# Weight pieces split three ahead from two raw buffers, and gate products turned through four PSUM banks

## The chip, the core and the metric

The kernel runs on one core of a Trainium2 chip. The metric is device time in microseconds (us) from launch to end. The engines are TensorE (PE, its weight loads PEld), VectorE (DVE), ScalarE (ACT), GpSimd (POOL) and SyncE (SP, which here only issues DMAs). Lines such as L1178 are lines of the kernel before.

## What is computed

The reference is one layer of a decoder block for 256 tokens and 2048 channels, in float32. After a projection by `w_in` come retention and dilated attention, merged by gates and `w_out`; then cross attention on 256 memory tokens; then an expert layer in which each token picks, for each of 8 heads, 16 of 16384 experts by product keys:

```python
def expert_block(args):
    x_, i_, g_ = args
    u = u_tab[i_]
    a = jax.nn.gelu(jnp.einsum('td,tkd->tk', x_, u), approximate=False)
    return jnp.einsum('tk,tkd->td', a * g_, v_tab[i_])
```

`u_tab` and `v_tab` have 16384 rows of 2048 channels. The result is normalized once more.

## The kernel before, in words

**The stream.** All weights come as a stream of 464 pieces of 128 x 4 x 512 float32 (1 MiB). Pieces 0 to 207 belong to the projections and the memory layer, 208 to 335 to the table u, 336 to 463 to the table v: the kernel does not gather the experts of 192 of its tokens, but multiplies all 16384 rows of u by the tokens (`u_chunk`, L904), takes the Gelu, multiplies by a dense matrix G of gates, and multiplies by all rows of v (`v_group`, L989). The other 64 tokens are done by gathering rows (`lanes`, L811): per row of 128 lanes an indirect DMA on POOL (L835) and one DVE instruction (L843 for u, L861 for v), three fetches ahead.

**How a piece is fed.** Float32 products are made from two float32r parts. A piece lands in one of `RAW_BUFS` = 3 buffers `raw`, by a DMA that SP issues (`load_to`, L1162). ACT casts it to `hi` (L1177), DVE subtracts `lo` = raw - hi (L1178). These two have three buffers each, as the pool `stream` has. Three matmuls per block (`mm3`, L210 to L212) use `hi`, `lo` and the split activations; where the 64 tokens are left out, two of them make the second half (L916, L917, L1026, L1027). A piece of the first kind has 24 matmuls, one of u or v 20. `ahead(n)` (L1170) splits up to piece n + 2 before piece n's matmuls are written, and behind each split of a piece i stands the load of piece i + 3.

**The order of the work** is the order in which this Python code issues it: every engine and every DMA queue runs its instructions in that order. Side work consists of generators. `tick()` (L126) lets each of them go on by credits; from the routing on it is called twice per piece, after the second block of matmuls and after the piece, so a tick is half a piece.

**Gate products.** `weigh` (L929) is such a generator. Its items are, for each of 32 chunks of 512 experts, one of kind "a" (128 tokens) and for every second chunk one of kind "b" (64 tokens, two chunks side by side). Per item it loads a block of G and a block of activations `act` on SP's queue (L939 to L944, five items ahead), multiplies them on DVE (L969, two steps ahead), transposes four blocks on TensorE into one PSUM bank (L974), casts the bank on ACT (L977, L981), and a step later subtracts on DVE (`low`, L950, L955), which empties the bank. The bank comes from the tag `tp`, which has two. The tag `sm` has two more, which other parts use earlier (attention, scores, the matrix G). The result is one buffer of the pool `units`, which has `N_UNITS` = 30 buffers of 4 KB for nearly everything. `v_group` waits until the results of its chunk are there. Results for the table v may run eight chunks ahead of it, and so they are made in bursts, from the last quarter of one group of v pieces into the next group.

**The start** (L1183 to L1203) loads and splits the first `RAW_BUFS` pieces by quarters (`quarters`, L1159), with the split of x's quarter i beside piece i, and x's last quarter after them.

Of the kernel before, what the change touches and what calls it, by code (L numbers as in the profile page):

```python
# [10 lines left out]
F32R = mybir.dt.float32r  # L11
# [9 lines left out]
KQ = 4  # L21
# [8 lines left out]
N_EXP = N_KEYS * N_KEYS  # L30
N_CH = N_EXP // 512
V_GROUPS = (4, 8, 8, 8, 4)
RAW_BUFS = 3
SPLIT_AHEAD = 2
N_UNITS = 30
LANES = slice(64, 128)
LOW = slice(0, 64)
TICK = 4.0
LOADS = 5
# [36 lines left out]
def block_kernel(ctx, tc, a, out):  # L76
    nc = tc.nc
    ctx.enter_context(tc.manual_schedule())
    cp = ctx.enter_context(tc.tile_pool(name="consts", bufs=1))
    st = ctx.enter_context(tc.tile_pool(name="stream", bufs=3))  # L80
    up = ctx.enter_context(tc.tile_pool(name="units", bufs=N_UNITS))
    wp = ctx.enter_context(tc.tile_pool(name="work", bufs=4))
    sp = ctx.enter_context(tc.tile_pool(name="small", bufs=2))
# [3 lines left out]
    def unit(shape, dt=F32):  # L87
        return up.tile([128] + shape, dt, tag="unit", name="unit")
# [4 lines left out]
    def bank(tag, shape):  # L93
        return ps.tile([128] + shape, F32, tag=tag, name=tag, bufs=4 if tag == "acc" else 2)
# [77 lines left out]
    def split_sb(raw, gi, kq, ks=range(4), into=None):  # L172

        hi, lo = into or (unit([4, T], F32R), unit([4, T], F32R))
        for k in ks:
            g = gains[:, gi, 4 * kq + k:4 * kq + k + 1]
            nc.scalar.activation(hi[:, k], raw[:, k], AF.Copy, scale=g)
            nc.vector.scalar_tensor_tensor(lo[:, k], raw[:, k], g, hi[:, k], op0=OP.mult, op1=OP.subtract)
        return hi, lo
# [69 lines left out]
    x_T = [None] * KQ  # L249
    sm = {}  # L250

    def load_xT(kq):
        raw = unit([4, T])
        nc.sync.dma_start(raw, a["xT"][kq])
        return raw
# [376 lines left out]
    hf_T = [None] * 4  # L632
# [268 lines left out]
    v_at = [0]  # L901
# [27 lines left out]
    def weigh():  # L929

        while len(g_done) < 2:
            yield
        items = [(kind, c) for c in range(N_CH) for kind in ("a", "b")[:1 + c % 2]]
        w, turned = {}, {}

        def load(kind, c):
            t = unit([2, 512])
            if kind == "a":
                nc.sync.dma_start(t[:, 0], G_d[0][:, c * 512:c * 512 + 512])  # L939
                nc.sync.dma_start(t[:, 1], ga.pop(c))  # L940
            else:
                nc.sync.dma_start(t[LOW, 0], G_d[1][:, c * 512 - 512:c * 512])
                nc.sync.dma_start(t[LANES, 0], G_d[1][:, c * 512:c * 512 + 512])
                nc.sync.dma_start(t[:, 1], gb.pop(c // 2))  # L944
            w[kind, c] = t

        def low(kind, c):
            o, tp = turned.pop((kind, c))
            if kind == "a":
                nc.vector.tensor_sub(o[:, 1], tp, o[:, 0])  # L950
                A_T[c] = o
            else:
                both = tp.rearrange("p k (c t) -> p c k t", c=2)
                for j in range(2):
                    nc.vector.tensor_sub(o[:, j, :, 64:128], both[:, j], o[:, j, :, 0:64])  # L955
                B_T[c // 2] = o

        yield
        yield
        for i in range(LOADS):  # L960
            load(*items[i])
        for i in range(-3, len(items) + 1):
            if 0 <= i - 1:
                low(*items[i - 1])
            while i + LOADS < len(items) and 0 <= i and items[i][1] > v_at[0] + (1 if hf_T[0] is not None else 8):
                yield
            if 0 <= i + 2 < len(items):
                t = w[items[i + 2]]
                nc.vector.tensor_mul(t[:, 1], t[:, 1], t[:, 0])  # L969
            if 0 <= i < len(items):  # L970
                t = w.pop(items[i])
                tp = bank("tp", [4, 128])
                for k in range(4):
                    nc.tensor.transpose(tp[:, k], t[:, 1, k * 128:k * 128 + 128], ident)  # L974
                o = unit([2, 4, 128], F32R)
                if items[i][0] == "a":
                    nc.scalar.copy(o[:, 0], tp)  # L977
                else:
                    both = tp.rearrange("p k (c t) -> p c k t", c=2)
                    for j in range(2):  # L980
                        nc.scalar.copy(o[:, j, :, 0:64], both[:, j])  # L981
                turned[items[i]] = o, tp
            if LOADS <= i + LOADS < len(items):
                while items[i + LOADS][1] not in ga and items[i + LOADS][0] == "a" or items[i + LOADS][0] == "b" and items[i + LOADS][1] // 2 not in gb:
                    yield
                load(*items[i + LOADS])
            yield
# [134 lines left out]
    def route():  # L1122
# [5 lines left out]
        yield from gate_matrix()  # L1128
    call(lambda: add(route()))
    call(lambda: add(weigh(), 1))  # L1130
    call(lambda: add(lanes_in()))

# [22 lines left out]
    stream = [e for e in prog if e[0] is not None]  # L1155
# [3 lines left out]
    def quarters(i):  # L1159
        return [slice(k, k + 1) for k in range(KQ)] if i <= RAW_BUFS else [slice(0, KQ)]  # L1160

    def load_to(m):  # L1162
        while at["load"] < min(m, len(stream)):
            i = at["load"]
            raws[i] = st.tile([128, KQ, 512], F32, name="raw", bufs=RAW_BUFS)
            for ks in quarters(i):
                nc.sync.dma_start(raws[i][:, ks], stream[i][0][:, ks])
            at["load"] += 1

    def ahead(n):  # L1170
        while at["split"] < min(n + SPLIT_AHEAD + 1, len(stream)):
            i = at["split"]
            load_to(i + RAW_BUFS)
            raw = raws.pop(i)
            hi, lo = st.tile([128, KQ, 512], F32R, name="hi"), st.tile([128, KQ, 512], F32R, name="lo")
            for ks in quarters(i):
                nc.scalar.copy(hi[:, ks], raw[:, ks])  # L1177
                nc.vector.tensor_sub(lo[:, ks], raw[:, ks], hi[:, ks])  # L1178
            parts[i] = (hi, lo)
            at["split"] += 1  # L1180
            load_to(i + 1 + RAW_BUFS)

    raw_x = []  # L1183
    for i in range(RAW_BUFS):
        raw_x.append(load_xT(i))
        raws[i] = st.tile([128, KQ, 512], F32, name="raw", bufs=RAW_BUFS)
        for k in range(KQ):
            nc.sync.dma_start(raws[i][:, k], stream[i][0][:, k])
    at["load"] = RAW_BUFS
    raw_x.append(load_xT(3))  # L1190
    for i in range(RAW_BUFS):
        raw = raws.pop(i)
        hi, lo = st.tile([128, KQ, 512], F32R, name="hi"), st.tile([128, KQ, 512], F32R, name="lo")
# [6 lines left out]
        parts[i] = hi, lo  # L1200
        at["split"] = i + 1
        load_to(i + 1 + RAW_BUFS)
    x_T[3] = split_sb(raw_x[3], 0, 3)  # L1203
    n = 0
    for ap, fn in prog:
        if ap is None:
# [99 lines left out]
```

## Time and profile before

| | |
|---|---|
| median of three runs | 2597.49 us (2588.37 to 2598.75) |
| the profiled execution, its own time | 2592.94 us |
| its span, first to last instruction | 2591.0 us |
| mean granted TensorE clock | 0.990 of full speed |
| bytes moved by DMA | 700.50 MB, 270 GB/s over the span |
| SBUF of `raw`, `hi`, `lo` and `units`, per partition | 9 x 8 KB and 30 x 4 KB |

The profile is of one execution. An engine is busy while it runs an instruction; waiting and issuing DMAs are not counted. In a row of grouped instructions stand line, engine, operation, tile written <- tiles read, count, then busy us and mean ns of one, then the engine's idle time just before them and what ended it. A wait reads "engine, line <- what ended it: us in total, times, longest". A row of DMA issues gives count, size and the median us from issue to landing.

### The profile page before, as it was taken

What the parts mean: (1) busy time and instruction counts of PE and PEld (TensorE: products, weight loads), DVE (VectorE), ACT (ScalarE), POOL (GpSimd) and SP (SyncE); (2) the same over time, 40 slices, a digit from 0 to 9 for tenths busy, and PEclk for the clock granted to TensorE, in tenths of its full rate; (3) what the DMA queues carried; (4) which work ended last, traced back from release to release, by engine and by line L of the source; (5) the groups of instructions that cost most, each with busy time, mean ns of one, the idle gap of its engine ahead of it and who ended that gap; (6) DMA issues with size and microseconds to landing.
All of it is one profiled execution on the core that took longest, in us unless ns stands there. A gap on an engine that the chain in (4) does not pass through costs nothing.

```text
span 2591.0 us, 29643 instructions
## 1 busy us (share of the span) xinstructions
PE 2497.3 (96%) x11426; PEld 2062.8 (80%) x11426; DVE 1874.5 (72%) x2168; ACT 1256.3 (48%) x1302; POOL 553.0 (21%) x361
## 2 busy tenths in 40 slices
PE   9999999999999999999989989999999899998998
PEld 7888888888888888888867768887877787876886
DVE  7566545787564344456889998887779888898984
ACT  6434334443355443454544458885554344443444
POOL 0211110001100000000023332323334454443621
PEclk9999999999999999999999999999999999999999
DMA  8555555567666554465569889999999999999984
GB/s 293 193 182 169 189 187 176 190 212 268 211 241 214 183 176 145 164 216 175 200 236 357 303 287 342 361 355 359 383 357 376 348 403 357 400 385 343 380 344 154
DMA packets 160141, 700.50 MB, mean 270 GB/s; under 512 B 15968, under 2 KB 40576, under 8 KB 101120
## 3 DMA queue, kind: packets, MB, share of 16 engines
q1 hardware_dynamic: 110352, 531.18, 57.6%
q0 software_dynamic: 42736, 154.85, 15.7%
q10 hardware_dynamic: 6912, 12.59, 1.3%
q8 instruction: 89, 1.46, 0.2%
q14 instruction: 52, 0.43, 0.0%
HBM read 666.01 MB, written 31.98 MB: 269 GB/s over the span
## 4 chain that ended last, share of the span: by engine, by line
PE 65%; DVE 11%; DMA 6%; issue 2%; ACT 1%; POOL 0%; SPq 0%; ACTq 0%; DVEq 0%; POOLq 0%
PE acc L211 16%; PE acc L212 16%; PE acc L210 16%; DVE lo L1178 5%; PE acc L1026 3%; PE acc L1027 3%; PE acc L916 3%; PE acc L917 3%; DMA unit<-G 2%; DMA raw<-in_v_dram 2%; DVE unit L843 2%; PE sm L772 2%; DMA unit<-act 1%; PE tp L193 1%; PE sm L594 1%
## 5 line engine op out<-in xcount | busy, mean ns | idle before, releaser
L1178 DVE TENSOR_TENSOR lo<-raw,hi 128x2048 fp32r<-128x2048 f32 (+1 forms) x464 | 1059.5, 2285 | 534.5 <-ACT hi L1177 533.5
L1177 ACT CAST hi<-raw 128x2048 fp32r<-128x2048 f32 (+1 forms) x464 | 880.2, 1900 | 665.9 <-PE acc L212 288.8
L211 PE MATMUL acc<-lo,unit 128*128 128x512 f32 x2688 | 1055.9, 393 | 33.9 <-DVE lo L1178 33.1
L210 PE MATMUL acc<-hi,unit 128*128 128x512 f32 x2688 | 1065.6, 396 | 6.5 <-ACT hi L1197 6.5
L212 PE MATMUL acc<-hi,unit 128*128 128x512 f32 x2688 | 1052.2, 391 | 0.0
L211 PEld LDWEIGHTS acc<-lo,unit 128*128 128x128 f32 x2688 | 508.2, 189 | 148.2 <-DVE lo L1178 47.4
L210 PEld LDWEIGHTS acc<-hi,unit 128*128 128x128 f32 x2688 | 508.0, 189 | 107.8 <-ACT hi L1197 7.0
L212 PEld LDWEIGHTS acc<-hi,unit 128*128 128x128 f32 x2688 | 507.8, 189 | 105.5
L835 POOL DMA_INDIRECT unit<-in_u_rows_dram,unit x128 | 216.4, 1691 | 446.8 <-DVE unit L843 157.6
L835 POOL DMA_INDIRECT unit<-in_v_rows_dram,unit x128 | 230.6, 1801 | 253.6 <-DVE unit L861 161.9
L1026 PE MATMUL acc<-hi,unit 128*128 128x512 f32 x512 | 201.7, 394 | 0.0
L1027 PE MATMUL acc<-lo,unit 128*128 128x512 f32 x512 | 201.3, 393 | 0.0
L916 PE MATMUL acc<-hi,unit 128*128 128x512 f32 x512 | 201.0, 393 | 0.0
L917 PE MATMUL acc<-lo,unit 128*128 128x512 f32 x512 | 200.6, 392 | 0.0
L861 DVE SCALAR_TENSOR_TENSOR unit<-unit 128x1024 f32<-128x1024 f32 x128 | 161.9, 1279 | 7.2 <-DMA unit<-xs 6.7
L843 DVE CUSTOM_DVE_ANT_0 unit<-unit 128x1024 f32<-128x1024 f32 x128 | 155.8, 1218 | 0.7 <-DMA unit<-in_u_rows_dram,unit 0.5
L1026 PEld LDWEIGHTS acc<-hi,unit 128*128 128x128 f32 x512 | 97.5, 190 | 21.1 <-DVE unit L955 0.2
L1027 PEld LDWEIGHTS acc<-lo,unit 128*128 128x128 f32 x512 | 97.4, 190 | 20.8
L916 PEld LDWEIGHTS acc<-hi,unit 128*128 128x128 f32 x512 | 97.3, 190 | 20.9
L917 PEld LDWEIGHTS acc<-lo,unit 128*128 128x128 f32 x512 | 97.1, 190 | 20.9
L342 POOL TENSOR_TENSOR unit<-work 128x512 f32<-128x512 f32 x20 | 37.7, 1884 | 176.4 <-DVE work L340 157.1
L169 POOL TENSOR_TENSOR rstd<-rstd2t,nhalf 128x2 f32<-128x2 f32 x1 | 0.7, 695 | 338.2 <-DVE rstd2t L163 338.2
(235 smaller groups left out, 1437.6 us busy)
## 6 DMA issues: line engine op xcount, KB each, us to landing
raw<-in_u_dram SPq DMA_DIRECT2D x128, 1024.0 KB, 6.9
raw<-in_v_dram SPq DMA_DIRECT2D x128, 1024.0 KB, 8.1
raw<-in_w_in_dram SPq DMA_DIRECT2D x96, 1024.0 KB, 4.9
raw<-in_w_kv_dram SPq DMA_DIRECT2D x32, 1024.0 KB, 4.9
raw<-in_w_out_dram SPq DMA_DIRECT2D x16, 1024.0 KB, 4.9
raw<-in_w_qm_dram SPq DMA_DIRECT2D x16, 1024.0 KB, 4.9
raw<-in_w_om_dram SPq DMA_DIRECT2D x16, 1024.0 KB, 4.9
raw<-in_w_pq_dram SPq DMA_DIRECT2D x16, 1024.0 KB, 4.9
```

What stands on the lines that cost most here:

```text
L210: nc.tensor.matmul(acc, lh, rh, start=start, stop=False)
L211: nc.tensor.matmul(acc, lh, rl, start=False, stop=False)
L212: nc.tensor.matmul(acc, ll, rh, start=False, stop=stop)
L835: nc.gpsimd.indirect_dma_start(rows[i], None, t, bass.IndirectOffsetOnAxis(ap=ix[:, j // 2, j % 2:j % 2 + 1], axis=0))
L843: nc.vector.tensor_tensor_reduce(r, r, hn[i % 2].rearrange("p a b -> p (a b)"), 1.0, 0.0, OP.mult, OP.add, dots[:, i // 2, i % 2:i % 2 + 1])
L861: nc.vector.scalar_tensor_tensor(y, r, coef[:, i // 2:i // 2 + 1], y, op0=OP.mult, op1=OP.add)
L916: nc.tensor.matmul(accs[1], th[:, k, 128:256], hi[:, k], start=first, stop=False)
L917: nc.tensor.matmul(accs[1], th[:, k, 128:256], lo[:, k], start=False, stop=last)
L1026: nc.tensor.matmul(accs[n][1], tb[:, k], hi[:, k], start=f, stop=False)
L1027: nc.tensor.matmul(accs[n][1], tb[:, k], lo[:, k], start=False, stop=e)
L1177: nc.scalar.copy(hi[:, ks], raw[:, ks])
L1178: nc.vector.tensor_sub(lo[:, ks], raw[:, ks], hi[:, ks])
```

## The change

- `RAW_BUFS` 3 to 2, `SPLIT_AHEAD` 2 to 3, the pool `stream` has 4 buffers of `hi` and of `lo` (formerly 3), `N_UNITS` 30 to 28.
- In `weigh` the cast out of PSUM is a stage of its own (`high`), one tick after the transposes; `low` follows one tick after it. The loop has one step more. The banks alternate between the tags `tp` and `sm`.
- At the start two pieces are loaded and split by quarters beside x's quarters 0 and 1 (`quarters` then takes in pieces 0 to 2), and x's quarters 2 and 3 are loaded and split after them.

```diff
-RAW_BUFS = 3
-SPLIT_AHEAD = 2
-N_UNITS = 30
+RAW_BUFS = 2
+SPLIT_AHEAD = 3
+N_UNITS = 28
...
-    st = ctx.enter_context(tc.tile_pool(name="stream", bufs=3))
+    st = ctx.enter_context(tc.tile_pool(name="stream", bufs=SPLIT_AHEAD + 1))
...
+        def high(kind, c):
+            o, tp = turned[kind, c]
+            if kind == "a":
+                nc.scalar.copy(o[:, 0], tp)
+            else:
+                both = tp.rearrange("p k (c t) -> p c k t", c=2)
+                for j in range(2):
+                    nc.scalar.copy(o[:, j, :, 0:64], both[:, j])
+
...
-        for i in range(-3, len(items) + 1):
-            if 0 <= i - 1:
-                low(*items[i - 1])
-            while i + LOADS < len(items) and 0 <= i and items[i][1] > v_at[0] + (1 if hf_T[0] is not None else 8):
+        for i in range(-3, len(items) + 2):
+            if 0 <= i - 2:
+                low(*items[i - 2])
+            if 0 <= i - 1 < len(items):
+                high(*items[i - 1])
+            while i + LOADS < len(items) and 0 <= i and items[min(i, len(items) - 1)][1] > v_at[0] + (1 if hf_T[0] is not None else 8):
                 yield
...
-                tp = bank("tp", [4, 128])
+                tp = bank("sm" if i % 2 else "tp", [4, 128])
                 for k in range(4):
                     nc.tensor.transpose(tp[:, k], t[:, 1, k * 128:k * 128 + 128], ident)
-                o = unit([2, 4, 128], F32R)
-                if items[i][0] == "a":
-                    nc.scalar.copy(o[:, 0], tp)
-                else:
-                    both = tp.rearrange("p k (c t) -> p c k t", c=2)
-                    for j in range(2):
-                        nc.scalar.copy(o[:, j, :, 0:64], both[:, j])
-                turned[items[i]] = o, tp
+                turned[items[i]] = unit([2, 4, 128], F32R), tp
...
-    raw_x.append(load_xT(3))
+    raw_x.extend(load_xT(i) for i in range(RAW_BUFS, KQ))
...
-    x_T[3] = split_sb(raw_x[3], 0, 3)
+    for i in range(RAW_BUFS, KQ):
+        x_T[i] = split_sb(raw_x[i], 0, i)
```

## Rows read from the trace of the kernel before

**Rows 1.** The page's first part: busy us, share, instructions, by engine.

```profile
PE 2497.3 (96%) x11426; PEld 2062.8 (80%) x11426; DVE 1874.5 (72%) x2168; ACT 1256.3 (48%) x1302; POOL 553.0 (21%) x361
```

**Rows 2.** Stretches: length, busy us (instructions) by engine, granted clock, DMA share, GB/s.

```profile
60.00:1253.00 1193.00, 1191.61 (x5540) 993.89 (x5539) 688.30 (x675) 519.96 (x526) 93.33 (x86) 1.00 0.56 194
1253.00:1555.00 302.00, 270.39 (x1130) 213.19 (x1129) 286.86 (x549) 145.85 (x123) 75.11 (x45) 0.98 0.79 283
1555.00:1765.00 210.00, 210.00 (x1105) 180.48 (x1104) 180.25 (x298) 186.18 (x310) 60.76 (x38) 1.00 0.98 350
1808.00:1926.00 118.00, 118.00 (x523) 97.70 (x521) 92.43 (x84) 61.42 (x45) 42.44 (x26) 1.00 0.99 378
2050.00:2141.00 91.00, 91.00 (x404) 75.34 (x403) 82.49 (x55) 38.30 (x20) 47.79 (x28) 1.00 1.01 404
2141.00:2193.00 52.00, 45.79 (x209) 36.66 (x208) 45.55 (x48) 21.75 (x24) 20.84 (x12) 0.93 1.01 356
2193.00:2303.00 110.00, 108.72 (x480) 89.70 (x479) 97.23 (x64) 45.95 (x24) 55.12 (x32) 1.00 1.00 395
2303.00:2374.00 71.00, 59.66 (x271) 47.27 (x270) 60.63 (x66) 28.42 (x33) 24.10 (x15) 0.93 0.98 349
2374.00:2528.00 154.00, 154.00 (x681) 127.56 (x680) 133.39 (x89) 71.38 (x46) 70.10 (x39) 1.00 0.93 361
2528.00:2578.00 50.00, 50.00 (x222) 41.23 (x220) 27.26 (x17) 23.25 (x23) 5.18 (x4) 1.00 0.42 147
```

**Rows 3.** TensorE's waits, first from 1253 to 1555 us, then 1927 to 2528.

```profile
PE acc L211 <- DVE lo L1178: 24.3, 16, 2.8
...
PE tp L974 <- DVE unit L950: 20.4, 16, 3.7
PE acc L211 <- DVE lo L1178: 8.8, 3, 6.0
PE tp L974 <- DVE unit L955: 5.9, 2, 4.0
```

**Rows 4.** The split's two instructions in the page's groups, and SP's longest wait.

```profile
L1178 DVE TENSOR_TENSOR lo<-raw,hi 128x2048 fp32r<-128x2048 f32 (+1 forms) x464 | 1059.5, 2285 | 534.5 <-ACT hi L1177 533.5
L1177 ACT CAST hi<-raw 128x2048 fp32r<-128x2048 f32 (+1 forms) x464 | 880.2, 1900 | 665.9 <-PE acc L212 288.8
...
SPq L1167 <- DVE lo L1178: 1673.0, 359, 13.3
```

**Rows 5.** Landings by stretch: 60:1253, 1350:1555, 1555:1765, 2050:2141, 2303:2374.

```profile
raw<-in_w_kv_dram SPq DMA_DIRECT2D x32, 1024.0 KB, 4.9
...
raw<-in_u_dram SPq DMA_DIRECT2D x38, 1024.0 KB, 6.0
...
raw<-in_u_dram SPq DMA_DIRECT2D x38, 1024.0 KB, 8.1
...
raw<-in_v_dram SPq DMA_DIRECT2D x21, 1024.0 KB, 8.3
...
raw<-in_v_dram SPq DMA_DIRECT2D x11, 1024.0 KB, 11.2
```

**Rows 6.** Groups of instructions: two from 2050 to 2141 us, one from 1253 to 1555.

```profile
L1177 ACT CAST hi<-raw 128x2048 fp32r<-128x2048 f32 x20 | 38.3, 1915 | 52.2 <-PE acc L1026 31.0 <-DMA raw<-in_v_dram 21.2
L861 DVE SCALAR_TENSOR_TENSOR unit<-unit 128x1024 f32<-128x1024 f32 x28 | 35.4, 1278 | 0.5 <-DMA unit<-in_v_rows_dram,unit 0.5
...
L1178 DVE TENSOR_TENSOR lo<-raw,hi 128x2048 fp32r<-128x2048 f32 x57 | 130.1, 2284 | 8.4 <-ACT hi L1177 8.1
```

**Rows 7.** Timeline of DVE: start us, us, instruction, [idle before it].

```profile
2363.23 0.69 DVE L969 TENSOR_TENSOR unit<-unit 128x512 f32<-128x512 f32 x1 [3.67 <-DMA unit<-act]
```

**Rows 8.** Timelines at the start: SP's load of piece 2, splits on DVE and ACT.

```profile
9.52 2.96 SPq L1188 DMA_DIRECT2D raw<-in_w_in_dram  x4
...
16.81 0.69 DVE L1198 TENSOR_TENSOR lo<-raw,hi 128x512 fp32r<-128x512 f32 x1
...
19.47 1.71 ACT L177 ACTIVATE unit<-unit,gains 128x256 fp32r<-128x256 f32 x4
```

## The prediction

> **What bounds the kernel now.** I read the totals first, then a table of stretches, then what TensorE waits for in them, and last the loop that feeds it. TensorE is busy in 96% of the span, DVE, next, in 72% [rows 1]: at most some 90 us of idle TensorE can be won, and any new wait that TensorE sees costs at once. The table [rows 2] shows three kinds of stretch. From 60 to 1253 us (projections, attention, memory layer) TensorE has no gap, and the DMA engines are 0.56 busy. From 1253 to 1555 us (routing) DVE is busy in 286.9 of 302 us, and TensorE idles 31.6. After 1765 us unbroken stretches of TensorE alternate with broken ones (2141 to 2193, 2303 to 2374 us), where the gate products are made; until 2528 us the DMA engines are 0.93 to 1.01 busy and move up to 404 GB/s.
>
> The waits say why it breaks [rows 3]. In routing TensorE waits 24.3 us for `lo`. From 1927 to 2528 us it waits 20.4 + 5.9 us for DVE to empty a PSUM bank of `weigh` (L950, L955), and 8.8 us for `lo`. These 59 us are what the change can remove.
>
> The loop that feeds TensorE: load a piece into `raw`, cast `hi` on ACT, subtract `lo` on DVE, load that `raw` buffer again. The cast takes 1.90 us, the subtraction 2.29; with hand-offs I count 4.3 us for a split. SP issues a load only when a `lo` is through: 1673 us of SP's waits are for L1178 [rows 4]. A piece of the two big tables is 20 matmuls; 20 casts in an unbroken 91 us [rows 2, 6] make 4.55 us a piece; one of 24 matmuls lasts 24/20 of that, 5.45 us. Now the landings [rows 5]: 4.9 us from the issue where nothing else moves, 6.0 in routing, 8.1 beside the gate matrix, 8.3 in an unbroken stretch beside the gathers of expert rows, and 11.2 in a broken one, behind `weigh`'s own loads.
>
> With three `raw` buffers the loop may last three pieces: (8.3 + 4.3)/3 = 4.2 us a piece, just under 4.55. That this is tight can be seen: from 2050 to 2141 us ACT sits 21.2 us before casts whose piece has not landed [rows 6]. TensorE has no gap there only because the splits run ahead.
>
> **The change, part by part.**
>
> *Two raw buffers, splits three ahead.* The load of piece n+5 still stands behind the split issued at piece n; formerly split n+2 freed one of three buffers, now split n+3 frees one of two. What moves is the deadline: the load has two pieces, not three, until its own split is due. In steady state the loop gives a piece every (landing + 4.3)/2. Four `hi`/`lo` buffers add a lead of one piece, 4.5 us, once; they don't raise the rate.
>
> - 60 to 1253 us: (4.9 + 4.3)/2 = 4.6 us, under 5.45: nothing. The cover is the 1.7 us per two pieces left over, and the lead.
> - Routing: DVE sets the pace, 302 us / 57 subtractions = 5.3 us a piece [rows 2, 6]; the loop needs (6.0 + 4.3)/2 = 5.15. No new wait; the lead saves 4.5 of the 24.3 us once.
> - 1555 to 1765 us (gate matrix): 210 us / 38 loads = 5.5 us a piece [rows 2, 5]. At 8.1 us the loop would need 6.2, at 6.0 us 5.15. I take nothing, since fewer loads in flight land sooner; upper end 38 x 0.7 = +26 us.
> - The unbroken stretches from 1808 to 2528 us are 118 + 91 + 110 + 154 = 473 us, 104 pieces [rows 2]. How soon a load lands when at most one other is in flight and gathers run, no row shows. Lower end: 4.9 us, a load alone, 4.6 us a piece, 104 x 0.05 = +5 us. Upper end: 8.3 us as now, 6.3 a piece, 104 x 1.75 = +182 us. I take 6.0 us, the landing in routing, because there gathers run already and DVE's pace spaces the loads out: 5.15 us a piece, 104 x 0.60 = **+62 us**. The DMA engines carry 4.55 now; it is the round trip through two buffers that would not.
> - 2528 to 2578 us, no gathers: 4.9 us, 11 x 0.05 = +1 us.
>
> The Trainium skill, in DMA: Bandwidth & Descriptors, section Anatomy of one DMA, gives a fixed 2.0 us plus bytes over 436 GB/s (for the gpsimd path), an estimate of 4.4 us for 1 MiB. By it the loop would take 4.35 us a piece and the +62 would be 0; the 4.9 us of the quiet stretch lie near it, the 8.3 us do not.
>
> While a cast waits for its load, ACT holds `weigh`'s `high` and the Gelu evictions behind it, DVE behind `lo` holds `low`, the products with gathered rows and the additions of L995, and SP behind the next load holds `weigh`'s loads. In the unbroken stretches none of these is due for several us; in the broken ones they are.
>
> *Weigh's stages and four banks.* `high` moves one tick (half a piece) later, `low` one more, and a transpose takes a bank last used four items ago instead of two. No instruction is added. The waits of 20.4 + 5.9 us would go. What is late next: DVE's product L969 waits up to 3.7 us for `act` to land [rows 7], and the `raw` loop. The broken stretches take 71 us / 11 loads = 6.5 us a piece [rows 2, 5]; at their landing of 11.2 us a two-buffer loop needs 7.75, for the 19 pieces in 52 + 71 us 19 x 1.25 = +24 us. Ends -26 and +24; I take **-13 us**, half the bank waits: these pieces give a load more time than the unbroken ones, but the same queue carries `weigh`'s loads.
>
> *Two units fewer.* From 2050 to 2141 us DVE waits 0.5 us for gathered rows [rows 6], so a gather that starts a little later is covered: 0. Without that cover each late gather would hold DVE, and with it `lo`.
>
> *The start.* Piece 2's load, issued at 9.5 us, now waits for the whole split of piece 0, and the splits of x 2 and 3 go ahead of piece 2's on ACT instead of beside it. They are eight slices at 0.43 us, of which the four of x 3 came after it: 4 x 0.43 = 1.7 us later than now. Piece 2's first quarter is subtracted by 17.5 us and its last some 3 us later, while TensorE still works on pieces 0 and 1 [rows 8]; ends 0 and the 3 us by which the load starts later, taken **+2 us**.
>
> **Sum:** +62 + 1 - 4.5 - 13 + 2 = +47 us on the profiled execution's 2592.9 us (its span of 2591.0 and 1.9 around it): **2640 us**. That execution lies 4.6 us (0.2%) under the median of the three runs.
>
> **Rivals.**
> - *Faster: loads come back quickly, and the waits go.* With at most two loads in flight one lands in 4.9 us even beside gathers: +5 + 1 + 2, all bank waits gone (-26), -4.5 in routing, half of the 8.8 us of late `lo`: -27 us, **2566 us**. It decides wherever a load lands under 2 x 4.55 - 4.3 = 4.8 us. For it: the 4.9 us [rows 5]. Against: 6.0 us in routing, where the DMA engines are only 0.79 busy [rows 2]. The page's formula above speaks for this one. Chance 0.20.
> - *Both cancel.* A landing of 5.4 us: loop 4.85, +31; with the bank waits gone and the rest as above about 0: **2593 us**. Chance 0.13.
> - *Much slower.* The landing stays at 8.3 us, because it is contention with the gathers and not the raw loads queued before it: +182 + 26 + 24 and -1 for the rest, **2824 us**. Waits of TensorE can add half clock: in the 71 us with 11.3 us of idle the granted clock was 0.93, elsewhere 1.00 [rows 2], between its levels of 1.2 and 2.4 GHz. Against: a slower TensorE thins the gathers too, since its pieces' ticks issue them. Chance 0.07.
>
> The same page says, under Queues, rings and completion order, that each DMA engine goes round the queues that have work, packet by packet; a raw load would then share with gathers however few raw loads wait, which speaks against the first rival.
>
> **How the numbers follow.** Forecast 0.60, rivals 0.20, 0.13 and 0.07. A measurement here can tell about 0.5% (13 us) from no change. Faster by more: the first rival, 0.20; within it 0.13; slower 0.67. The forecast's own range is 2615 to 2715: landings of 5.5 to 7.0 us make +36 to +114 for the 104 pieces, and at the upper end half of the +24 stands in place of the -13. To hold 8 in 10 the range takes in the second rival and the slower half of the first, and leaves the last out: 2575 to 2715.
>
> **What would show it.** Right: from 1808 to 2528 us casts follow about 5.1 us apart; ACT's wait for `raw` is the largest before L1177, its wait for TensorE nearly gone; TensorE waits for `lo` some 50 us or more there; raw landings fall to about 6 us; transposes no longer wait for L950 and L955; 60 to 1253 us is unchanged. Wrong: landings near 4.9 us with TensorE unbroken (first rival) or unchanged at 8 (last), or the time going to routing, which would mean that late casts held DVE there.

## The result, and the profile after

The changed kernel takes 2754.84 us (median of 4 runs, 2748.41 to 2761.64) against 2595.89 us before in the same comparison: ratio 1.0625, 95% interval 1.0606 to 1.0645. It is slower by 159 us; 2640 us was forecast. The profiled execution took 2748.41 us, with a span of 2746.3. The ratios, here and below, are worked out from the single executions of both kernels and need not be the quotient of the medians. One execution of the kernel with six half buffers, at a granted clock of 0.846, took 2804.59 us and is left out of its numbers.

Lines have moved: the cast `hi` is L1181 now, the subtraction `lo` L1182, the loads L1171; in `weigh` the product is L980, the transposes L985, `high` L950 and L954, `low` L959 and L964; the v matmuls are L1030 and L1031. From the profile's page after: the totals, the chain by engine, the chain by line, and the split's two groups [rows 1, 4].

```profile
PE 2537.2 (92%) x11426; PEld 2074.5 (76%) x11426; DVE 1875.6 (68%) x2165; ACT 1254.7 (46%) x1299; POOL 500.8 (18%) x361
...
PE 36%; DMA 25%; DVE 16%; ACT 7%; issue 5%; POOL 1%; ACTq 0%; DVEq 0%; POOLq 0%; SPq 0%
DMA raw<-in_v_dram 12%; DMA raw<-in_u_dram 11%; PE acc L211 11%; PE acc L212 11%; PE acc L210 11%; DVE lo L1182 10%; ACT hi L1181 6%; DMA unit<-in_v_rows_dram,unit 1%; DVE unit L861 1%; DVE unit L843 1%; PE tp L193 1%; DMA unit<-G 1%; PE sm L594 1%; PE sm L625 1%; POOL unit L342 0%
...
L1182 DVE TENSOR_TENSOR lo<-raw,hi 128x2048 fp32r<-128x2048 f32 (+1 forms) x465 | 1060.6, 2281 | 723.9 <-ACT hi L1181 722.5
L1181 ACT CAST hi<-raw 128x2048 fp32r<-128x2048 f32 (+1 forms) x465 | 882.5, 1899 | 1016.6 <-DMA raw<-in_v_dram 384.4
```

The work is the same: DVE, ACT and the matmuls are as many and nearly as long. TensorE's idle time grew from 94 to 209 us (span less busy), and its busy time by 40 us, as after its gaps it ran more often at 1.2 instead of 2.4 GHz (mean granted clock 0.975, formerly 0.990). DVE and ACT are idle longer too, so no engine became the bound. The chain that ended last was 65% PE and 6% DMA before; now it is 36% PE, and 23% are landings of raw pieces. ACT's largest wait before a cast is a load, no longer TensorE.

The table of stretches after [rows 2]: projections to memory layer, routing, gate matrix, and then the first three of the stretches that were unbroken and broken in turn (1862, 1986 and 2117 us are where 1817, 1926 and 2046 us were):

```profile
60.00:1265.00 1205.00, 1194.63 (x5538) 995.41 (x5538) 690.65 (x682) 527.28 (x535) 95.34 (x86) 1.00 0.56 194
1265.00:1581.00 316.00, 272.43 (x1131) 215.89 (x1131) 288.37 (x547) 144.52 (x121) 70.76 (x44) 0.96 0.77 270
1581.00:1805.00 224.00, 216.51 (x1113) 184.78 (x1112) 176.89 (x293) 182.13 (x301) 54.47 (x36) 0.98 0.94 324
1862.00:1986.00 124.00, 113.17 (x488) 89.84 (x487) 82.12 (x74) 55.16 (x41) 34.65 (x26) 1.00 0.87 320
1986.00:2117.00 131.00, 103.99 (x462) 84.50 (x460) 103.71 (x123) 48.83 (x45) 31.97 (x22) 0.88 0.91 318
2117.00:2232.00 115.00, 101.00 (x425) 77.85 (x425) 84.52 (x55) 40.13 (x21) 46.45 (x30) 1.00 0.89 321
```

No stretch behind the gate matrix is unbroken now. From 2117 to 2232 us, which was gapless, TensorE idles 14 of 115 us, and the DMA engines move 321 GB/s where they moved 404: the DMA engines are less busy (0.89, before 1.01), not fuller. The groups of that stretch for ACT [rows 6], ACT's timeline from 2150 to 2172 us, and the landings of the stretch [rows 5] show the loop:

```profile
L1181 ACT CAST hi<-raw 128x2048 fp32r<-128x2048 f32 x21 | 40.1, 1911 | 77.3 <-DMA raw<-in_v_dram 71.4 <-DVE unit L861 3.6 <-DVE lo L1182 2.3
```

```profile
2151.09 1.91 ACT L1181 CAST hi<-raw 128x2048 fp32r<-128x2048 f32 x1 [6.09 <-DMA raw<-in_v_dram]
2157.31 1.91 ACT L1181 CAST hi<-raw 128x2048 fp32r<-128x2048 f32 x1 [4.31 <-DMA raw<-in_v_dram]
2162.45 1.92 ACT L1181 CAST hi<-raw 128x2048 fp32r<-128x2048 f32 x1 [3.23 <-DMA raw<-in_v_dram]
2168.71 1.91 ACT L1181 CAST hi<-raw 128x2048 fp32r<-128x2048 f32 x1 [4.34 <-DMA raw<-in_v_dram]
```

```profile
raw<-in_v_dram SPq DMA_DIRECT2D x22, 1024.0 KB, 6.5
```

Casts are 5.1 to 6.3 us apart, each just behind its landing, while TensorE wants a piece every 4.54 us. TensorE's waits from 1804 to 2734 us [rows 3]:

```profile
PE acc L211 <- DVE lo L1182: 55.9, 50, 1.9
PE sm L985 <- DVE unit L980: 31.0, 8, 8.3
PE acc L1030 <- DVE unit L964: 18.1, 1, 18.1
PE tp L985 <- DVE unit L980: 11.6, 6, 3.9
```

The waits of 20.4 + 5.9 us for a bank are gone, as the change meant. In their place transposes wait 42.6 us for the products that they turn, and TensorE once waits 18.1 us for a `low`.

Routing shows another wait. Before (1253 to 1555 us) and after (1265 to 1581 us), with L739 the transposes of the gates and L732 and L719 the routing products that they turn:

```profile
PE acc L211 <- DVE lo L1178: 24.3, 16, 2.8
PE tp L739 <- DVE unit L732: 6.4, 2, 3.5
...
PE acc L211 <- DVE lo L1182: 25.9, 19, 2.7
PE tp L739 <- DVE unit L732: 13.0, 2, 9.0
PE tp L739 <- DVE unit L719: 4.2, 1, 4.2
```

The wait for `lo` has hardly grown; the transposes wait 17.2 us instead of 6.4.

### The profile page after: what moved, and what is told of

Its sections match the earlier page's. It is cut to its first block, busy times and chain, and to the rows that moved or that the text cites. A ratio compares the mean times of both kernels' runs of the same rounds, so it can differ in the third digit from the quotient of the medians.

```text
span 2746.3 us, 29699 instructions
## 1 busy us (share of the span) xinstructions
PE 2537.2 (92%) x11426; PEld 2074.5 (76%) x11426; DVE 1875.6 (68%) x2165; ACT 1254.7 (46%) x1299; POOL 500.8 (18%) x361
## 4 chain that ended last, share of the span: by engine, by line
PE 36%; DMA 25%; DVE 16%; ACT 7%; issue 5%; POOL 1%; ACTq 0%; DVEq 0%; POOLq 0%; SPq 0%
DMA raw<-in_v_dram 12%; DMA raw<-in_u_dram 11%; PE acc L211 11%; PE acc L212 11%; PE acc L210 11%; DVE lo L1182 10%; ACT hi L1181 6%; DMA unit<-in_v_rows_dram,unit 1%; DVE unit L861 1%; DVE unit L843 1%; PE tp L193 1%; DMA unit<-G 1%; PE sm L594 1%; PE sm L625 1%; POOL unit L342 0%
## 5 line engine op out<-in xcount | busy, mean ns | idle before, releaser
L1182 DVE TENSOR_TENSOR lo<-raw,hi 128x2048 fp32r<-128x2048 f32 (+1 forms) x465 | 1060.6, 2281 | 723.9 <-ACT hi L1181 722.5
L1181 ACT CAST hi<-raw 128x2048 fp32r<-128x2048 f32 (+1 forms) x465 | 882.5, 1899 | 1016.6 <-DMA raw<-in_v_dram 384.4
L835 POOL DMA_INDIRECT unit<-in_u_rows_dram,unit x128 | 194.1, 1516 | 529.2 <-DVE unit L843 215.1
L835 POOL DMA_INDIRECT unit<-in_v_rows_dram,unit x128 | 198.8, 1553 | 355.7 <-DVE unit L861 291.9
L1030 PE MATMUL acc<-hi,unit 128*128 128x512 f32 x512 | 204.6, 400 | 18.1 <-DVE unit L964 18.1
L1031 PE MATMUL acc<-lo,unit 128*128 128x512 f32 x512 | 203.8, 398 | 0.0
L1030 PEld LDWEIGHTS acc<-hi,unit 128*128 128x128 f32 x512 | 98.9, 193 | 40.2 <-issue 18.5
L1031 PEld LDWEIGHTS acc<-lo,unit 128*128 128x128 f32 x512 | 98.9, 193 | 21.8
L772 PE MATMUL sm<-unit 128*128 128x128 f32 x384 | 52.3, 294 | 15.6 <-ACT unit L773 15.6
```

The source lines that it names most:

```text
L835: nc.gpsimd.indirect_dma_start(rows[i], None, t, bass.IndirectOffsetOnAxis(ap=ix[:, j // 2, j % 2:j % 2 + 1], axis=0))
L1030: nc.tensor.matmul(accs[n][1], tb[:, k], hi[:, k], start=f, stop=False)
L1031: nc.tensor.matmul(accs[n][1], tb[:, k], lo[:, k], start=False, stop=e)
```

## The experiments

Each run has a ledger made from its trace: the time between the first matmuls of pieces, against the trace of before, in us. "Unbroken" are the four stretches of pieces 312 to 335, 356 to 376, 392 to 408 and 422 to 451 (92 pieces, 417.8 us before, 4.54 each); "broken" the 48 pieces between them; "gate" the pieces 266 to 311 (gate matrix and first product). The start is pieces 0 to 29, routing 226 to 265. From 30 to 225 no run differs by over 3 us, and at pieces 452 to 463 none by over 5. A ledger is of one execution, the profiled one, which can lie off the median of its kernel: 16 us under it for "two raw, split three ahead, old weigh", 12 us over it for "the change, split two ahead". A small difference between two rows is therefore no result by itself.

| kernel | median us (ratio) | start | routing | gate | unbroken | broken |
|---|---|---|---|---|---|---|
| before, length in us | 2594.4 | 177.2 | 211.5 | 261.8 | 417.8 | 288.9 |
| the change | 2754.8 (1.0625) | +12.0 | +13.7 | +19.3 | +82.9 | +23.0 |
| two raw, split two ahead, old weigh, 30 units | 2749.5 (1.0615) | +6.1 | +12.8 | +15.3 | +96.5 | +18.1 |
| two raw, split three ahead, old weigh, 28 units | 2747.5 (1.0601) | +10.8 | +13.4 | +15.6 | +72.9 | +22.5 |
| the change, split two ahead | 2764.4 (1.0652) | +6.1 | +21.3 | +29.8 | +88.1 | +32.9 |
| before with weigh's new stages and banks | 2589.8 (0.9982) | -0.2 | +2.3 | -0.3 | +0.8 | -3.8 |
| the change in half buffers | 2661.0 (1.0267) | +4.4 | +6.4 | -1.3 | +30.0 | +26.0 |
| the change without gathers | 2618.6 (1.0109) | +11.8 | +3.2 | -4.5 | +15.3 | -7.9 |
| new weigh, four raw, 28 units | 2657.4 (1.0238) | -0.9 | +2.6 | +1.8 | +46.0 | +18.5 |
| before with 28 units | 2654.2 (1.0227) | -1.1 | +2.7 | -0.5 | +42.8 | +23.0 |
| four half buffers, split two ahead, 32 units | 2663.5 (1.0261) | +0.4 | +9.1 | -0.7 | +38.3 | +29.4 |
| the same, 28 units | 2672.8 (1.0309) | +1.1 | +9.0 | -1.2 | +50.0 | +17.9 |
| six half buffers, new weigh, 30 units | 2598.3 (1.0015) | -1.0 | +6.6 | -1.1 | +9.5 | -9.3 |
| before, 28 units, weigh's loads three ahead | 2685.1 (1.0347) | -0.9 | 0.0 | +10.7 | +17.0 | +68.9 |

### The change taken apart

At first three theories stood against each other: that the raw loop alone is the cost (A), that a good part comes from side work standing behind a split that is issued a piece earlier (B), and that weigh's new stages are late (C). The profile after had suggested B, since TensorE's longest waits lie where it hands work to DVE.

**Two raw buffers alone**, in the kernel before (three `hi` and `lo`, 30 units):

```diff
-RAW_BUFS = 3
+RAW_BUFS = 2
...
-    raw_x.append(load_xT(3))
+    raw_x.extend(load_xT(i) for i in range(RAW_BUFS, KQ))
...
-    x_T[3] = split_sb(raw_x[3], 0, 3)
+    for i in range(RAW_BUFS, KQ):
+        x_T[i] = split_sb(raw_x[i], 0, i)
```

> The kernel before with two raw buffers and the start's edit that goes with them; splits still two ahead, weigh as before, 30 units. Theory A (the loop through two raw buffers alone costs the time: it gives a piece every (landing 6.4 to 7 + 4.5)/2 = 5.5 us where TensorE wants 4.55): nearly all of the +159 us is here already, and a bit more since the lead is one piece shorter: 2750 to 2790 us. Theory B (a good part comes from splits three ahead, behind which ACT and DVE hold the side work that TensorE waits for at every hand-off; in the changed kernel those stalls at the edges add up to some 50 to 70 us): 2685 to 2720 us. Theory C (weigh's new stages are late, not the raw loop): below 2650 us.

2749.48 us, ratio 1.0615 (1.0584 to 1.0646): the whole loss is here, with weigh as before, so theory C is out.

**The change with weigh as before** (two raw, splits three ahead, 28 units):

```diff
-                tp = bank("sm" if i % 2 else "tp", [4, 128])
+                tp = bank("tp", [4, 128])
...
-                turned[items[i]] = unit([2, 4, 128], F32R), tp
+                o = unit([2, 4, 128], F32R)
+                if items[i][0] == "a":
+                    nc.scalar.copy(o[:, 0], tp)
...
+                turned[items[i]] = o, tp
```

> The changed kernel with weigh's cast, subtraction and banks as before; two raw buffers, splits three ahead, 28 units. Theory A: the lead of one piece more saves 5 to 20 us against two raw buffers with splits two ahead: 2735 to 2775 us. Theory B: 2745 to 2780 us, some 50 us above the kernel with two raw buffers and splits two ahead. Theory C: below 2670 us.

2747.54 us, ratio 1.0601 (1.0578 to 1.0624), 2 us under the run before it, where theory B wanted 50 us more.

**The change with splits two ahead:**

```diff
-SPLIT_AHEAD = 3
+SPLIT_AHEAD = 2
```

> The changed kernel with splits two ahead (three hi and three lo buffers) and all else as changed. Theory A: no better than the changed kernel, 2755 to 2780 us. Theory B: the stalls at the edges shrink: 2685 to 2725 us; TensorE's waits for weigh's products L980 and for the transposes fall by over half. Theory C: as the changed kernel, 2745 to 2765 us.

2764.38 us, ratio 1.0652 (1.0629 to 1.0676): 10 us more than the change, with intervals that overlap. Theory B has fallen as an account of the loss: over the whole kernel the earlier split does not cost; that it gives a little back is not shown. It holds in two places. At the start TensorE waits 8.8 us for L193's operand with splits three ahead (60 to 170 us) and 3.6 us with splits two ahead; the start's column says the same (12.0 and 6.1). In routing the earlier split trades one wait for another: in the four kernels with splits three ahead and two raw buffers (whole or as halves) TensorE waits 19.2 to 25.9 us for `lo` and 16.6 to 17.9 us at L739, in the four with splits two ahead 28.8 to 36.7 us for `lo` and 5.7 to 8.6 us at L739.

**Weigh's stages and banks alone**, in the kernel before: `high`, the step more and the alternating banks of the change's diff, and nothing else.

> The kernel before with weigh's later cast and subtraction and its four banks, and nothing else: three raw buffers, splits two ahead, 30 units. Theories A and B: the waits of 20.4 + 5.9 us for a bank go and something else is late next, so 2570 to 2596 us; waits of transposes for the subtraction vanish from the list. Theory C: slower than before, 2620 us or more.

2589.83 us, ratio 0.9982 (0.9967 to 0.9997), the one version under the kernel before, by 4.5 us, which is only just clear of the noise (the profiled execution is 1 us under). TensorE's waits from 1920 to 2620 us, against 20.4, 8.8 and 5.9 [rows 3]:

```profile
PE acc L211 <- DVE lo L1182: 14.9, 4, 10.3
PE tp L985 <- DVE unit L980: 9.2, 5, 3.4
PE acc L1030 <- DVE unit L964: 8.1, 1, 8.1
PE sm L985 <- DVE unit L980: 3.9, 4, 1.9
```

The bank waits vanish, and 36 us of waits remain of 35. What a broken stretch lacks is not a bank: in all four lines TensorE waits for DVE, where products, `low` and splits follow each other, and another of them is late in place of the one that was listed.

### What makes a raw load slow, and what a shorter loop gives

**The change without gathers.** `fetch` gathers only the first two rows, and each later step reuses them:

```diff
             if i < 256:
+                if i >= 2:
+                    rows[i] = rows[i % 2]
+                    return
                 rows[i] = unit([1024])
...
-            r = rows.pop(i)
-            nc.vector.tensor_tensor_reduce(r, r, hn[i % 2].rearrange("p a b -> p (a b)"), 1.0, 0.0, OP.mult, OP.add,
+            r = rows[i]
+            nc.vector.tensor_tensor_reduce(junk, r, hn[i % 2].rearrange("p a b -> p (a b)"), 1.0, 0.0, OP.mult, OP.add,
...
-            r = rows.pop(128 + i)
+            r = rows[128 + i]
```

> The changed kernel without all gathers of expert rows but the first two, which every later step reuses; the DVE work on them stays, and the 64 tokens' expert sum is not the reference's. What the gathers do to the landings: Theory A1 (a raw load is slowed by the gathers' packets): landings in the four unbroken stretches fall from 6.5 to 5 us, pieces from 5.45 to 4.9 or less, 92 x 0.55 = 50 us less there and 10 to 25 us in the gate matrix and routing: 2670 to 2700 us. Theory A2 (two raw loads in flight slow each other, the gathers hardly): landings stay over 6 us, 2740 to 2760 us.

2618.56 us, ratio 1.0109 (1.0081 to 1.0138), less than even A1 gave. The landings of the whole execution, first of the change, then of this run:

```profile
raw<-in_u_dram SPq DMA_DIRECT2D x128, 1024.0 KB, 6.4
raw<-in_v_dram SPq DMA_DIRECT2D x128, 1024.0 KB, 6.8
```

```profile
raw<-in_u_dram SPq DMA_DIRECT2D x128, 1024.0 KB, 5.1
raw<-in_v_dram SPq DMA_DIRECT2D x128, 1024.0 KB, 4.9
```

With the same two buffers, raw loads land 1.3 and 1.9 us sooner, and the unbroken stretches lose 15.3 instead of 82.9 us. By the loop, (4.9 + 4.4)/2 = 4.65 us a piece; measured 4.71. So the loss is the length of the loop, and what lengthens it is the gathers. It is not the buffers that they give back: in the change DVE waits only 6.9 us for rows of v. Whether a gather costs a raw load its time in the DMA engines or elsewhere was not tested. The broken stretches become 7.9 us shorter than before.

**Half buffers.** The same bytes of `raw` as four buffers of 512 KB, each loaded, cast and subtracted by itself:

```diff
-            raws[i] = st.tile([128, KQ, 512], F32, name="raw", bufs=RAW_BUFS)
+            raws[i] = [st.tile([128, 2, 512], F32, name="raw", bufs=2 * RAW_BUFS) for _ in range(2)]
...
-            for ks in quarters(i):
-                nc.scalar.copy(hi[:, ks], raw[:, ks])
-                nc.vector.tensor_sub(lo[:, ks], raw[:, ks], hi[:, ks])
+            for h in range(2):
+                for ks in steps(i):
+                    to = slice(2 * h + ks.start, 2 * h + ks.stop)
+                    nc.scalar.copy(hi[:, to], raw[h][:, ks])
+                    nc.vector.tensor_sub(lo[:, to], raw[h][:, ks], hi[:, to])
```

> The changed kernel, but each raw buffer is two half buffers of 512 KB with a load, a cast and a subtraction of their own, so that a load starts when half a split is through; the bytes of raw are the same. Theory A (length of the loop through two buffers): half a split is some 2.3 us, a half load lands in 3.3 to 6.5 us, so the loop can give a piece every 2.8 to 4.4 us, under the 4.53 that TensorE takes; the four unbroken stretches lose 80 us, the gate matrix some 15 to 20, the broken ones 10 to 20: 2610 to 2660 us. Theory D (the DMA engines are full, and a piece takes 5.5 us whatever waits for it; or the order behind the splits is what costs): 2730 to 2780 us.

2660.99 us, ratio 1.0267 (1.0242 to 1.0292): 94 us come back, a trifle short of what theory A gave; theory D is out. The gate column loses its +19.3 altogether. But 66 us remain, and the half loads are hardly quicker than the change's whole ones (6.4 and 6.8 us):

```profile
raw<-in_u_dram SPq DMA_DIRECT2D x256, 512.0 KB, 6.3
raw<-in_v_dram SPq DMA_DIRECT2D x256, 512.0 KB, 7.1
```

Only the split's part of the loop was shortened, and not to half: in the three formerly unbroken stretches of v a half load lands in 6.5 to 6.7 us in the mean, and from the start of its cast to the end of its subtraction pass 2.9 to 3.5 us, because DVE begins the subtraction 0.6 to 1.2 us after the cast. By the loop, (6.6 + 2.9)/2 to (6.6 + 3.5)/2 = 4.75 to 5.05 us a piece; measured 4.82 to 5.05, still over 4.54.

### Two units fewer

**The kernel before with 28 units:**

```diff
-N_UNITS = 30
+N_UNITS = 28
```

> The kernel before with 28 units in place of 30 and nothing else. If units have slack, as the prediction took: 2588 to 2600 us. If two units fewer delay weigh's loads or gathers: 2605 us or more.

2654.16 us, ratio 1.0227 (1.02 to 1.0253): 59 us for what the prediction priced at nothing. Waits of DVE from 1920 to 2620 us, and its work on gathered rows from 2050 to 2141 us [rows 6]:

```profile
DVE unit L861 <- DMA unit<-in_v_rows_dram,unit: 89.2, 46, 4.8
DVE lo L1178 <- ACT hi L1177: 26.6, 18, 3.1
```

```profile
L861 DVE SCALAR_TENSOR_TENSOR unit<-unit 128x1024 f32<-128x1024 f32 x24 | 30.8, 1283 | 22.0 <-DMA unit<-in_v_rows_dram,unit 22.0
L211 PE MATMUL acc<-lo,unit 128*128 128x512 f32 x72 | 29.1, 404 | 6.9 <-DVE lo L1178 6.9
```

DVE waits 89.2 us for gathered rows, 0.5 before. A row that comes late holds the subtraction behind it, that holds TensorE, and by the loop the next load: in pieces 356 to 376 a split takes 8.9 us in the mean instead of 5.1, a load 7.1, and three raw buffers give a piece every (7.1 + 8.9)/3 = 5.3 us; measured 5.12, before 4.55. The rows come late because they are asked for late: the gathers themselves land in 9.6 us, sooner than before (10.3).

**Four raw buffers and 28 units**, with weigh's new stages (`RAW_BUFS` 3 to 4, `N_UNITS` 30 to 28; all four quarters of x beside the first four pieces):

> The kernel before with weigh's later stages and four banks, four raw buffers and 28 units, splits two ahead. Theory A: three raw buffers carry the unbroken stretches already, so a fourth gives only what the broken stretches, the gate matrix and the start wait for raw: 2575 to 2592 us. Rival E (more loads in flight land later and take turns with weigh's loads and the gathers): 2592 to 2610 us.

2657.44 us, ratio 1.0238 (1.0213 to 1.0264). Neither theory had the units in it. ACT waits only 10.3 us for v pieces from 1920 to 2720 us (98.3 before), and the time is that of 28 units: DVE waits 87.8 us for v rows.

**Half buffers with 32 and with 28 units**, splits two ahead (`SPLIT_AHEAD` 3 to 2 in the half-buffer kernel, `N_UNITS` 28 to 32 or as it was):

> The changed kernel with half buffers (four of 512 KB), splits two ahead (three hi and lo buffers) and, in the room that this frees, 32 units. Theory F (two causes, each enough alone: the loop through two raw buffers, and two units fewer, which make gathers late so that DVE waits for their rows): both are gone, 2585 to 2605 us, DVE waits under 5 us for gathered rows. Theory G (what the halves left over, 66 us, is still the raw loop, now with half loads landing in 7 us): 2630 to 2665 us.

> As the run with half buffers and 32 units, but with 28 units. Theory F: as the kernel before with 28 units, 2645 to 2665 us, DVE waits 20 to 90 us for gathered rows. Theory G: the same as with 32 units, within 10 us.

2663.46 us (1.0233 to 1.0288) and 2672.77 us (1.0281 to 1.0337). DVE waits 12.1 and 31.8 us for v rows. Theory F is out and G holds: four units more give some 9 us beside half buffers, not clear of the noise (the intervals overlap, and the two profiled executions took the same time), so what is left is still the raw loop.

**Six half buffers**, the bytes of before (`RAW_BUFS` 3, 30 units, new weigh):

> Half buffers, six of them (the bytes of three raw buffers), splits two ahead, weigh's later stages and four banks, 30 units: the kernel before with halves and banks. Theory F: the loop has ample room, 2578 to 2592 us. Theory G: no better than 2590 us, since the loop through three buffers was enough; what the halves add (a second cast and subtraction per piece, some 0.1 us each) makes routing 0 to 10 us longer: 2590 to 2602 us.

2598.25 us, ratio 1.0015 (0.9999 to 1.0031), as theory G had it: nothing is won by halves where the loop has room, and routing grows by 6.6 us. Against the run with four half buffers and 32 units, the bytes of a third raw buffer are what was added (and two units taken away): 65 us. This is the plainest sign that the halves had left the raw loop too long.

**28 units, and weigh's loads three items ahead:**

```diff
-N_UNITS = 30
+N_UNITS = 28
...
-LOADS = 5
+LOADS = 3
```

> The kernel before with 28 units, and weigh's loads three items ahead instead of five, which gives two units back. Theory F with weigh's early loads as the holders: DVE's wait for gathered rows falls from 89 to under 20 us and the time to 2590 to 2615 us, with somewhat longer waits for G and act. If other holders bind (results of weigh made ahead, the rows themselves): 2640 to 2670 us.

2685.07 us, ratio 1.0347 (1.0323 to 1.0371): slower, though the step that was named came true. From 1920 to 2680 us:

```profile
DVE unit L969 <- DMA unit<-actb: 85.5, 13, 10.8
DVE lo L1178 <- ACT hi L1177: 62.2, 53, 3.1
DVE unit L969 <- DMA unit<-act: 27.9, 13, 4.8
```

No wait for gathered rows is left, and three of the four unbroken stretches are as long as before (0.0 each; the last +17.0). So two units taken from weigh's early loads are enough for the gathers. But its products now wait 113 us for their operands, and the broken stretches pay 68.9 us.

## Why the prediction was right in direction and wrong in size

The forecast of +47 us was too small by 108 us, against the profiled execution's +155. The raw loop accounts for 21 of them, the gate matrix for 19, routing for 18, the broken stretches for 36, the start for 10 and the end for 3. The mechanism, a loop of two buffers that is too slow, was the right one. The step that failed first is that it was priced only where nothing broke the stream, and there too low, and taken as nothing, or as less than the gain, in the gate matrix, in routing and in the broken stretches: two raw buffers alone cost 96.5 us in the unbroken stretches and 15.3, 12.8 and 18.1 us in those three.

- **The raw loop, +62 us.** The mechanism was right: most of its signs came as listed (casts behind landings, ACT's largest wait a load, TensorE waiting 55.9 us for `lo`). The term was mis-sized. It measured +82.9 us: 92 pieces, 0.90 us each, where 104 at 0.60 were counted. In these stretches the mean landing is 6.3 to 6.8 us instead of 6.0, and the mean from the start of the cast to the end of the subtraction 4.3 to 4.6, with 0.1 to 0.3 us before the cast; about (6.5 + 4.6)/2 = 5.55 us a turn. "I take 6.0 us, the landing in routing" failed. 6.0 us is the median of that row, while a loop adds up means, and the mean of the same loads is 6.5 us: with it the sum would have been (6.5 + 4.3)/2 = 5.4 us a piece and +88 us. That it would have come so near is in part luck, since routing and the unbroken stretches differ in traffic: 41 gathers in routing's 205 us, one every 5.0 us, against one every 3.4 to 4.7 in the unbroken stretches. How far the landings of that row spread, the kernel before shows. Those of 1350 to 1400 us, where gathers are densest, and below them those of 1450 to 1500 us are

```profile
raw<-in_u_dram SPq DMA_DIRECT2D x9, 1024.0 KB, 8.1
unit<-in_u_rows_dram,unit POOLq DMA_INDIRECT x17, 10.4
...
raw<-in_u_dram SPq DMA_DIRECT2D x10, 1024.0 KB, 5.4
unit<-in_u_rows_dram,unit POOLq DMA_INDIRECT x7, 8.2
```

With 17 gathers in 50 us a piece lands in 8.1 us, with 7 in 5.4. The number of gathers alone does not order the landings, though: the two other parts of the row have 5.6 us with 10 gathers in 50 us and 7.1 us with 9 in 55.
- **By the Trainium skill's formula** (DMA: Bandwidth & Descriptors, Anatomy of one DMA), which it states for the gpsimd path and whose estimate was 4.4 us, this term was 0. The loads here, which SP issues, lie 0.5 to 0.7 us above it in the quiet stretch and without gathers (4.9 to 5.1 us), and 2.0 to 2.4 us beside gathers (6.4 to 6.8). In the Trainium skill, the same page's section Queues, rings and completion order has the rule that each engine goes round the queues it has work for, packet by packet. The trace agrees with sharing: taking gathers away shortened raw loads, with the same two raw buffers. That the turn goes by packets no run here shows.
- **Gate matrix, 0 us.** It measured +19.3, inside the named upper end of 26. "Fewer loads in flight land sooner" was true by 0.9 us only, 7.2 instead of 8.1; with a split of 4.5 the loop of some 5.9 us is over the 5.5 us a piece.
- **Routing, -4.5 us.** It measured +13.7. Two things failed. The split was taken at 4.3 us, but here DVE, busy with routing, starts a subtraction 0.8 us after its cast, and the split takes 5.0; with a landing of 6.2 the loop is 5.6, over 5.3 us a piece. With splits two ahead this is seen as TensorE's wait for `lo`: 36.7 us instead of 24.3 with two raw buffers alone. And the lead of four `hi` and `lo` buffers, put at a gain of 4.5 us, won some 10 us of that wait and lost them again: by the order of issue the split of one more piece stands on DVE before the routing products, and the transposes L739 wait 17.2 us for these instead of 6.4. The prediction had this among its signs of being wrong ("late casts held DVE there"), but not in its sum.
- **Broken stretches, -13 us.** They measured +23.0. "Half the bank waits" was the failing step: with three raw buffers all of them vanish and the broken stretches win 3.8 us, because a bank was only the latest of several things due from DVE. The +24 us for the loop, put at the range's end, was near by luck: it counted 19 pieces in two stretches, and the third, 1926 to 2050 us, which stands in neither the rows nor the sum, makes 10.6 of the 23.0 us. A wait in a list can be won only down to the next one behind it.
- **Two units, 0 us.** The result looks as priced, but for another reason: alone the step costs 59 us. "DVE waits 0.5 us for gathered rows, so a gather that starts a little later is covered" failed; a wait near zero says that rows came in time, not by how much. In the change the cost does not show: there DVE waits 6.9 us for v rows, and gathers land in 8.0 us instead of 10.3. That pieces paced by the raw loop ask for rows more slowly would explain it, but is not shown apart. The two causes don't add: 155 us for two raw buffers alone, 59 us for the units alone, 159 for both.
- **The start, +2 us.** +12.0; with splits two ahead +6.1. What was priced, a late piece 2, measured nothing: up to piece 11 the change is not behind. The loss comes between the first matmuls of pieces 11 and 14. That the third split on ACT and DVE comes before the first side work, which TensorE's transposes (L193) then wait for, was not counted; the granted clock also falls, to 0.97 over the start (1.00 before).
- **The rivals.** The faster one needed landings under 4.8 us; they were 6.5. The much slower one kept 8.3 us as contention with the gathers; without gathers landings fall to 4.9 us, but with two buffers instead of three to 6.5 already, so both the gathers and the number of raw loads count. "None of these is due for several us" was right of the first pieces of a stretch; when the lead is used up, everything behind a split is due.

The ledger's other entries, +0.3 between the start and routing and +3.5 at the end, were taken at 0 and +1. Why half loads beside gathers take as long as whole ones was not taken apart further. Two readings of the prediction were off without moving its forecast: the granted clock was 0.93 in both broken stretches of the rows and 0.98 in routing, not 1.00 "elsewhere", and the upper end of its own range adds up to 2717 us.

## What to carry to other kernels

A ring of buffers passes one piece per (landing + time to free a buffer)/buffers; work it out for each stretch with the mean landing under its own traffic and with the split's own waits in it, and ask what lead the next buffers hold only after this rate is above the consumer's. A wait of nearly zero for a resource is not slack: taking away buffers of a shared pool is priced only by asking how many of them the fastest user has in flight and who holds the rest. Where two limits lie this near each other, test each edit alone, since the second hides behind the first.

## What the runs showed of the hardware that was not expected

A load of 512 KB is hardly quicker than one of 1 MiB where other queues are busy: 6.3 and 7.1 us beside gathers (u and v) against 6.4 and 6.8. In the quiet part (60 to 1265 us), where the two halves of a piece are issued about 1.1 us apart, it takes 4.3 us for the pieces of `w_in` and `w_kv`, up to 4.8 for others, against 4.9. By the formula of the Trainium skill, DMA: Bandwidth & Descriptors, section Anatomy of one DMA, which is stated for the gpsimd path, an estimate for 512 KB is 3.2 us, which no run here shows. The time to land also goes with the number of buffers, and so of loads in flight: in pieces 356 to 376 a whole load lands in 8.2 us in the mean with three buffers and in 6.3 with two, a half load in 6.7 us with four half buffers and in 9.5 with six, and with six TensorE loses nothing there. Gathers make raw loads slower (6.4 and 6.8 us with them, 5.1 and 4.9 without). The other way round it is only seen together: with raw loads thinned by the two-buffer loop, and gathers with them, the gathers of v rows fell from 10.3 to 8.0 us.
